# Scratch tensors in DRAM re-ordered by chunk and by head: convolved blocks, second mixer's queries and keys, attention values

## The chip, the cores and the metric

The kernel runs on one core of one Trainium2 chip. The metric is device time in microseconds (us) of one execution, the median of several; less is better. The profile is of one execution of its own, so its time stands beside the median below.

## What is computed

Two layers (`DEPTH = 2`) of a hybrid backbone, with the same weights for 128 context tokens and 1024 latent tokens. Each layer normalises, projects, runs three mixers side by side, projects back, and ends in a SwiGLU:

```python
u = rms_norm(x) * (1 + scale1) + shift1
(aq, ak, av, bq, bk, bv, bg, ba, bb, cq, ck, cv, co, ci, cf) = split(u @ w_in + b_in)
qkv = silu(centred_dwconv(concat([bq, bk, bv]), conv_w))        # 5 taps
a = diff_attention(rope(aq), [rope(ak), cached k], [av, cached v])   # 4 heads, two maps each
d = gated_delta(l2_norm(dq) / 8, l2_norm(dk), dv, beta, g)      # both directions, chunked
m = mlstm(cq, ck / 8, cv, ig, lf)                               # both directions, chunked
x += gate1 * (concat([norm(a), norm(d) * silu(bg), sigmoid(co) * norm(m)]) @ w_out)
x += gate2 * swiglu(rms_norm(x) * (1 + scale2) + shift2)
```

It returns both token streams and, for the context tokens, keys, values and the mixers' last states. Everything is float32 outside; every large product is made of three fp32r products of a high and a low part.

## The kernel before

Tokens are columns: 1152 of them (`NT`), 1024 latent and 128 context, in three groups `g` of 384 (`GW`) for the matmuls and in nine chunks of 128 (`NCH = 9`, the ninth is the context) for the mixers. A tile has 128 partitions.

Between the projections and the mixers the data goes through scratch tensors in DRAM, opened per layer in `open_s`. Three of them are the change's:

- `BT`, the convolved q, k, v blocks, `[P, 6, CVO]`: for each of 128 partitions six blocks of 1156 columns. `blk_b` (L727) stores one block `b` per call, a row of 4624 B per partition. `prep1` (L754) loads one chunk of all six blocks, six pieces of 512 B per partition. `delta_step` (L1062) loads one chunk of the first four blocks, four pieces of 512 B per partition, for either direction.
- `CQK`, queries and keys of the mLSTM mixer, `[P, 4, NT]`. `blk_c` (L746) stores block `b`, group `g`: 1536 B per partition. `prep1` (L756) loads a chunk of four blocks, four pieces of 512 B; `mlstm_step` (L1149) loads the two query blocks of a chunk, two pieces of 512 B.
- `VD`, attention values, `[10, P, 512]`: ten tiles of 128 keys by 4 heads of 128. `tok_cols` (L565) stores 256 columns (two heads) of one key tile, 1024 B per partition; `attn_consts` (L924) stores the cached values the same way. `attention` (L1231) loads one head: ten pieces of 512 B per partition.

Counts for both layers: L727 12 times, L746 24, L565 and L924 together 40; L754 and L756 18 each, L1062 and L1149 32 each, L1231 8.

The stages of a layer, in the order of the code: `tok_cols` 0 and the gates; `blk_b` and `blk_c`, ten blocks, in the first layer beside the modulation weights `aw`; `prep1` per chunk (transposes, decay matrices, stores of `RD`, `ND`, `RM`, `VK`); `inverse`; `prep2`, which loads `ND` (tile `w`, L851), finishes the triangular inverses and stores them into `RD` (L911); `blk_a` (attention's q and k, stored into `QD` and `KD`); the other `tok_cols`; then `mixers`: the scan (`delta_step`, `mlstm_step`, `merge`) beside `attention` (per head two loads of `K`, 640 KB each, one of `V`, 640 KB, and per 256 queries two of `Q`), `w_out`, and the feed-forward part.

Nearly all DMAs of the scratch are issued by SyncE (SP) in one queue, in order; weights `wr` are issued by ScalarE. The order of instructions on each engine is not that of the code: the program is built with

```python
with _tile.TileContext(nc, schedule_with_timeline_sim=True) as tc:
```

so that a planner, at build time, places every instruction by its own estimate of when operands come, and the chip then runs each engine's list as it stands. In the trace the stages above overlap: `prep1` begins among the blocks, `blk_a` and the later `tok_cols` run beside `prep1`, and attention's first scores (L1250) come among the last steps of `prep2`, ahead of the scan.

Of the kernel before, what the change touches and what calls it, by code (L numbers as in the profile page):

```python
# [17 lines left out]
P = 128  # L18
D = 1024
KB = 8  # L20
NL = 1024
NC = 128
NT = NL + NC
NG = 3
GW = 384
# [3 lines left out]
H = 4  # L29
EPS = 1e-6  # L30
NCH = 9
CVW = 1160
CVO = 1156
# [33 lines left out]
def cpos(c):  # L67
    return 128 * c if c < 8 else 1028


class Kern:
# [362 lines left out]
    def open_s(self, l):  # L434

        S = self.S = {}
        dt = lambda n, shape: self.dr.tile(shape, F32, name=f"{n}{l}")
        S["BT"] = dt("BT", [P, 6, CVO])
        S["CQK"] = dt("CQK", [P, 4, NT])
        S["V1"] = dt("V1", [NCH, P, H, 65])  # L440
        S["BC"] = dt("BC", [NCH, P, 512])
        S["QD"] = dt("QD", [8, 2, 64, NT])
        S["KD"] = dt("KD", [2, 2, 2, P, NT + P])
        S["VD"] = dt("VD", [10, P, 512])
        S["ND"] = dt("ND", [2, NCH, P, H, P])
        S["RD"] = dt("RD", [2, NCH, P, 1024])
        S["GR"] = dt("GR", [2, 16, NT])
        S["VK"] = dt("VK", [NCH, P, 768])
        S["RM"] = dt("RM", [2, NCH, P, 768])
        S["CAT"] = dt("CAT", [KB, P, NT])  # L450
        ed, pe = ExitStack(), ExitStack()
        self.dn = ed.enter_context(self.pool("psdn", PSUM))
        self.pp = pe.enter_context(self.pool("pspp", PSUM))
        return ed, pe
# [69 lines left out]
    def tok_cols(self, l, u, i, pr):  # L524

        nc, A, S = self.nc, self.A, self.S
        gb = GB if i else 10
        if i == 0:
            W = self.pre
            wd = 288  # L530
            sl = lambda w, k: w[k // 3][:, 288 * (k % 3):288 * (k % 3) + 288]
            off = 1024
            self.G = self.mx.tile([P, NCH, 32], F32, name=self.nm("G"))
        else:
            W = [self.load_w(A["w_tok"][l, i - 1, j]) for j in range(2)]
            wd = 256
            sl = lambda w, k: w[k // 4][:, 256 * (k % 4):256 * (k % 4) + 256]
            off = 256 * (i - 1)
        Wh, Wl = [w[0] for w in W], [w[1] for w in W]
        bt = self.t(pr, [P, GW], "gw", gb)  # L540
        nc.sync.dma_start(bt[:, :wd], A["btok"][l:l + 1, off:off + wd].to_broadcast([P, wd]))
        for tt in range(NCH):
            g, j = divmod(tt, 3)
            cs = slice(128 * j, 128 * j + 128)
            ps = self.ps(self.pp, "pp", 6) if i == 0 and 1 < tt < 8 else self.ps(self.dn, "dn", 2)
            o = ps[:, :wd]
            for k in range(KB):
                self.mm3(o, u[g][k][0][:, cs], u[g][k][1][:, cs], sl(Wh, k), sl(Wl, k), k == 0, k == KB - 1)
            if i == 0:
                v1 = self.t(pr, [P, GW], "gw", gb)[:, :260].rearrange("p (h v) -> p h v", h=H)  # L550
                nc.gpsimd.memset(v1[:, :, 64:65], 1.0)
                nc.vector.tensor_add(v1[:, :, 0:64], ps[:, :256].rearrange("p (h v) -> p h v", h=H),
                                     bt[:, 0:256].rearrange("p (h v) -> p h v", h=H))
                nc.sync.dma_start(S["V1"][tt], v1)
                nc.vector.tensor_add(self.G[:, tt, :], ps[:, 256:288], bt[:, 256:288])
            else:
                v = self.t(pr, [P, GW], "gw", gb)[:, :256]
                nc.vector.tensor_add(v, o, bt[:, :256])  # L558
                if i > 2:
                    nc.sync.dma_start(S["BC"][tt, :, off - 512:off - 256], v)  # L560
                    yield
                    continue
                if tt == 8:
                    nc.sync.dma_start(self.O["v"][l, :, off:off + 256], v)
                nc.sync.dma_start(S["VD"][tt if tt < 8 else 9, :, off:off + 256], v)  # L565
            yield

    def softplus(self, pool, z, shape):

# [135 lines left out]
    def blk_b(self, l, b, u):  # L705

        nc, S, pr = self.nc, self.S, self.pr
        w = self.load_w(self.A["w_st"][l, b])
        raw = self.t(self.cv, [P, CVW], "cv", 4)
        for lo, hi in ((0, 2), (1026, 1030), (1158, 1160)):  # L710
            nc.vector.memset(raw[:, lo:hi], 0.0)
        bias = self.p(l, "bst")[:, b:b + 1]
        for g in range(NG):
            ps = self.ps(self.dn, "dn", 2)
            self.block(ps[:, :GW], w, u[g])
            for lo, hi, cnd in self.ranges(g):
                o = 2 + GW * g + lo + (4 if cnd else 0)
                nc.scalar.activation(raw[:, o:o + hi - lo], ps[:, lo:hi], AF.Identity, bias=bias)
        cw = self.cwh[l]
        acc = self.t(self.cv, [P, CVW], "cv", 4)  # L720
        a = acc[:, :CVO]
        nc.vector.tensor_scalar(out=a, in0=raw[:, 0:CVO], scalar1=cw[:, 5 * b:5 * b + 1], scalar2=None, op0=ALU.mult)
        for j in range(1, 5):
            nc.vector.scalar_tensor_tensor(out=a, in0=raw[:, j:j + CVO], scalar=cw[:, 5 * b + j:5 * b + j + 1], in1=a, op0=ALU.mult, op1=ALU.add)
        nc.scalar.activation(raw[:, :CVO], a, AF.Tanh)
        nc.vector.scalar_tensor_tensor(out=a, in0=raw[:, :CVO], scalar=1.0, in1=a, op0=ALU.add, op1=ALU.mult)
        nc.sync.dma_start(S["BT"][:, b, :], a)  # L727
        if b < 4:
            sq = raw
            nc.scalar.activation(sq[:, :CVO], a, AF.Square)  # L730
            ps = self.ps(self.pp, "pp", 6)
            for c in range(NCH):
                nc.tensor.matmul(ps[:, 2 * c:2 * c + 2], lhsT=sq[:, cpos(c):cpos(c) + 128], rhs=self.hsel, start=True, stop=True)
            nc.vector.tensor_copy(self.ss[:, :, 2 * b:2 * b + 2], ps[:, :18].rearrange("p (c i) -> p c i", i=2))

    def blk_c(self, l, b, u):
        nc, S, pr = self.nc, self.S, self.pr
        w = self.load_w(self.A["w_st"][l, 6 + b])
        bias = self.p(l, "bst")[:, 6 + b:7 + b]
        for g in range(NG):  # L740
            ps = self.ps(self.dn, "dn", 2)
            self.block(ps[:, :GW], w, u[g])
            o = self.t(pr, [P, GW], "gw", GB)
            nc.scalar.activation(o, ps[:, :GW], AF.Identity, bias=bias)
            c = slice(GW * g, GW * g + GW)
            nc.sync.dma_start(S["CQK"][:, b, c], o)  # L746

    def prep1(self, l, c, c1):

        nc, S, pr, pp = self.nc, self.S, self.ch, self.pp  # L750
        o = slice(cpos(c), cpos(c) + 128)
        oc = slice(128 * c, 128 * c + 128)
        q6 = self.t(self.cv, [P, CVW], "cv", 4)[:, :768].rearrange("p (a t) -> p a t", t=128)
        nc.sync.dma_start(q6, S["BT"][:, :, o])  # L754
        c4 = self.t(c1, [P, 4, 128], "c4", 1)
        nc.sync.dma_start(c4, S["CQK"][:, :, oc])  # L756
        cq, ck = c4[:, 0:2], c4[:, 2:4]

        b4 = lambda a, w=64: a[:, :, None].to_broadcast([P, H, w])
# [13 lines left out]
        for d in range(2):  # L773
            e = self.t(c1, [P, 768], "em", EB)
# [13 lines left out]
        for d in range(2):  # L788
            gr = self.t(c1, [2, 8, 128], "gr", 2, F32R)
            nc.sync.dma_start(gr.bitcast(F32), S["GR"][:, 8 * d:8 * d + 8, oc])  # L790
            for x in range(2):
# [6 lines left out]
                if x == 0:  # L798
# [6 lines left out]
                    for b in range(4):  # L805
                        s = slice(32 * b, 32 * b + 32)
# [107 lines left out]
    def attn_consts(self, l):  # L914
        nc, pr, S, A = self.nc, self.pr, self.S, self.A
        for hf in range(2):
            ck = self.t(pr, [P, GW], "gw", GB)[:, :256].rearrange("p (b t) -> p b t", b=2)
            nc.sync.dma_start(ck, A["ckT"][l][:, hf])
            for p in range(2):
                self.put_k(hf, p, slice(NL, NL + P), ck[:, p, :], P)  # L920
        for i in range(2):
            cv = self.t(pr, [P, GW], "gw", GB)[:, :256]
            nc.sync.dma_start(cv, A["cv"][l][:, 256 * i:256 * i + 256])
            nc.sync.dma_start(S["VD"][8, :, 256 * i:256 * i + 256], cv)  # L924
        self.nlam = self.nlams[l]

    def put(self, dst, src, w):
# [118 lines left out]
    def delta_step(self, l, cs, S0, S1, seen):  # L1046
# [12 lines left out]
        if S0 is not None:  # L1059
            qk = self.t(sc, [P, 2, 4, 128], "qk", 2)  # L1060
            for d in range(2):
                nc.sync.dma_start(qk[:, d], S["BT"][:, 0:4, cpos(cs[d]):cpos(cs[d]) + 128])  # L1062
            pk = self.ps(pz, "z", 2)
            for d in range(2):
                for p in range(2):
# [60 lines left out]
    def mlstm_step(self, l, cs, C0, C1, seen):  # L1126
# [4 lines left out]
        for d in range(2):  # L1131
# [14 lines left out]
            nd = hv(nf)  # L1146
            if C0 is not None:
                cq = self.t(sc, [P, 2, 128], "cq", 3)
                nc.sync.dma_start(cq, S["CQK"][:, 0:2, 128 * c:128 * c + 128])  # L1149
                pq = self.ps(pz, "y", 1)  # L1150
                for p in range(2):
                    nc.tensor.matmul(pq[:, 130 * p:130 * p + 130], lhsT=cq[:, p, :], rhs=C0[:, d, p, :], start=True, stop=True)
# [58 lines left out]
    def attention(self, l):  # L1211
# [11 lines left out]
        for h in range(H):  # L1223
# [4 lines left out]
                nc.sync.dma_start(k.bitcast(F32), S["KD"][h // 2].rearrange("l p r t -> (l p) r t")[:, r:r + 32, :])  # L1228
                K.append(k)
            V = self.t(at, [P, 10, 128], "V", 2)  # L1230
            nc.sync.dma_start(V, S["VD"][:, :, 128 * h:128 * h + 128].rearrange("s p e -> p s e"))  # L1231
            for q0 in range(0, NT, 256):
                nq = min(256, NT - q0)
                q = self.t(at, [P, 2, 2, 256], "Q", 2, F32R)
# [319 lines left out]
```

## Time and profile before

| | us |
|---|---|
| median of 3 runs | 3792.27 (3789.85 to 3796.47) |
| the profiled execution | 3797.68 |
| its span, first to last instruction | 3795.9 |
| TensorE (PE) matmul busy in the span | 3540.6 (93%) |
| VectorE (DVE) busy | 2295.8 (60%) |
| ScalarE (ACT) busy | 1136.6 (30%) |
| GpSimd (POOL) busy | 654.4 (17%) |
| mean granted TensorE clock | 0.954 of 2.4 GHz |

Besides the page, four views of the trace are read: a table of busy times by stretch of time; the waits of an engine, by who ended them; instructions of one engine in order of time; and the DMA queues in a stretch. An issuing instruction of a DMA on SP is shown with the time that SP spent on it; the transfer itself comes after. "Packets" are the pieces that the 16 DMA engines moved, among them 16 of under 512 B for each DMA that tell of its end.

### The profile page before, as it was taken

The numbers are of one execution on the slowest core, as the hardware profiler recorded it, in microseconds if no ns is written. First come the engines' busy times: TensorE is split into PE (matmuls) and PEld (weight loads), VectorE is DVE, ScalarE is ACT, GpSimd is POOL, SyncE is SP. The second block draws the span as 40 slices with busy tenths as digits, with TensorE's granted clock in tenths as the row PEclk, the third lists the DMA queues.
The fourth block names the chain that finished last, engine by engine and source line by source line (L and its number), as shares of the span: only waits on it lengthen the run. The fifth ranks groups of instructions, "written<-read, shape, count | busy, mean of one in ns | idle before, by whom it ended". The sixth has DMA issues, their size and how long they took to land. (4 is left out here: it accounts for less than half of the span.)

```text
span 3795.9 us, 59415 instructions
## 1 busy us (share of the span) xinstructions
PE 3540.6 (93%) x22770; PEld 3369.8 (89%) x22770; DVE 2295.8 (60%) x5361; ACT 1136.6 (30%) x2383; POOL 654.4 (17%) x903
## 2 busy tenths in 40 slices
PE   7999978997899999999999997898789999999998
PEld 6997777886899999999989877788778999999997
DVE  7896677787455566654485567477775434333435
ACT  5323315445241111111243431244553311111111
POOL 2014232355020000000020324034632000000001
PEclk8999988999999999999999999889999999999999
DMA  5377624774212222221133663467542111111111
GB/s 215 128 247 234 217 78 124 225 214 132 92 59 84 78 81 81 95 78 48 59 110 99 221 230 97 132 175 205 137 140 66 34 39 41 49 40 39 51 45 56
DMA packets 277091, 434.13 MB, mean 114 GB/s; under 512 B 24648, under 2 KB 186504, under 8 KB 276552
## 3 DMA queue, kind: packets, MB, share of 16 engines
q1 hardware_dynamic: 247576, 324.29, 27.3%
q10 hardware_dynamic: 29232, 106.05, 8.7%
q8 instruction: 180, 2.95, 0.3%
q14 instruction: 103, 0.84, 0.1%
HBM read 315.85 MB, written 114.39 MB: 113 GB/s over the span
## 5 line engine op out<-in xcount | busy, mean ns | idle before, releaser
L362 DVE SCALAR_TENSOR_TENSOR x<-pd,mod,x 128x256 f32<-128x256 f32 (+1 forms) x832 | 405.2, 514 | 597.5 <-PE pd L191 596.3
L183 ACT CAST wh<-wr 128x1024 fp32r<-128x1024 f32 (+1 forms) x219 | 229.1, 1047 | 880.3 <-PE pu L190 462.2
L184 DVE TENSOR_TENSOR wl<-wr,wh 128x1024 fp32r<-128x1024 f32 (+1 forms) x219 | 267.6, 1228 | 173.6 <-ACT wh L183 173.1
L189 PE MATMUL pd<-hh,wh 128*128 128x384 f32 x1056 | 358.8, 340 | 7.3 <-DVE x L362 5.1
L189 PE MATMUL pg<-uh,wh 128*128 128x384 f32 x1056 | 357.2, 338 | 2.6 <-ACT uh L342 2.6
L190 PE MATMUL pg<-ul,wh 128*128 128x384 f32 x1056 | 357.9, 339 | 1.4 <-DVE ul L347 1.4
L299 POOL TENSOR_TENSOR nacc<-nacc,nsq 128x384 f32<-128x384 f32 x48 | 52.1, 1086 | 1769.6 <-issue 1572.7
L190 PE MATMUL pu<-ul,wh 128*128 128x384 f32 x1056 | 355.7, 337 | 0.0
L189 PE MATMUL pu<-uh,wh 128*128 128x384 f32 x1056 | 355.6, 337 | 0.0
L190 PE MATMUL pd<-hl,wh 128*128 128x384 f32 x1056 | 354.9, 336 | 0.0
L191 PE MATMUL pg<-uh,wl 128*128 128x384 f32 x1056 | 354.7, 339 | 0.0
L191 PE MATMUL pd<-hh,wl 128*128 128x384 f32 x1056 | 353.7, 336 | 0.0
L191 PE MATMUL pu<-uh,wl 128*128 128x384 f32 x1056 | 350.7, 337 | 0.0
L189 PE MATMUL dn<-uh,wh 128*128 128x384 f32 x864 | 300.1, 347 | 5.8 <-ACT gw L956 4.4
L190 PE MATMUL dn<-ul,wh 128*128 128x384 f32 x864 | 299.0, 346 | 0.0
L191 PE MATMUL dn<-uh,wl 128*128 128x384 f32 x864 | 298.2, 345 | 0.1
L1250 PE MATMUL s<-K,Q 128*128 128x384 f32 (+1 forms) x800 | 226.3, 393 | 58.6 <-DVE e L1251 23.7
L1251 DVE TENSOR_SCALAR_CACHE_REDUCE e<-s 128x384 f32<-128x384 f32 (+1 forms) x400 | 209.8, 539 | 67.8 <-PE s L1250 64.6
L189 PEld LDWEIGHTS pd<-hh,wh 128*128 128x128 f32 x1056 | 198.4, 188 | 18.6 <-issue 7.7
L189 PE MATMUL dn<-wh,uh 128*128 128x256 f32 (+1 forms) x624 | 186.2, 298 | 26.2 <-DVE gw L558 19.8
L1250 PEld LDWEIGHTS s<-K,Q 128*128 128x128 f32 x800 | 138.3, 207 | 78.8 <-DVE e L1251 39.0
L189 PEld LDWEIGHTS pg<-uh,wh 128*128 128x128 f32 x1056 | 199.5, 189 | 4.5 <-ACT uh L342 2.8
(354 smaller groups left out, 8221.6 us busy)
## 6 DMA issues: line engine op xcount, KB each, us to landing
wr<-in_w_gu_dram ACTq DMA_DIRECT2D x88, 512.0 KB
aw<-in_w_mod_dram SPq DMA_DIRECT2D x96, 256.0 KB
wr<-in_w_dn_dram ACTq DMA_DIRECT2D x44, 512.0 KB
wr<-in_w_st_dram ACTq DMA_DIRECT2D x36, 512.0 KB
rd<-RD SPq DMA_DIRECT2D x36, 512.0 KB
aw<-in_w_mod_dram SPq DMA_DIRECT2D x32, 512.0 KB
Q<-QD SPq DMA_DIRECT2D x64, 256.0 KB
RM<-em SPq DMA_DIRECT2D x36, 384.0 KB
```

Source lines behind the costliest of these rows:

```text
L183: nc.scalar.copy(hi, r)
L184: (eng or nc.vector).tensor_tensor(out=lo, in0=r, in1=hi.bitcast(F32), op=ALU.subtract)
L189: mm(out, lhsT=wh, rhs=xh, start=start, stop=False)
L190: mm(out, lhsT=wh, rhs=xl, start=False, stop=False)
L191: mm(out, lhsT=wl, rhs=xh, start=False, stop=stop)
L299: (nc.gpsimd if k in PST else nc.vector).tensor_tensor(out=self.acc[g], in0=self.acc[g], in1=s, op=ALU.add)
L362: nc.vector.scalar_tensor_tensor(out=x[g][k][:, lo:hi], in0=ps[:, lo:hi], scalar=gate[:, k, cnd:cnd + 1], in1=x[g][k][:, lo:hi], op0=ALU.m ...
L1250: nc.tensor.matmul(p[:, :w], lhsT=q[:, m, hl, 128 * j:128 * j + 128], rhs=K[m][:, 128 * ks[0]:128 * ks[0] + w], start=hl == 0, stop=hl == 1)
L1251: nc.vector.tensor_scalar(out=e[:, GW * i:GW * i + w], in0=p[:, :w], scalar1=0.125, scalar2=None, op0=ALU.mult, op1=ALU.max, accum_out=mx[ ...
```

## The change

The three scratch tensors get the order in which they are loaded: `BT` and `CQK` by chunk first, `VD` by head first. Each load then takes one unbroken row per partition: 3072 B (L754), 2048 B (L756 and L1062), 1024 B (L1149), 5120 B (L1231). Each store is cut: a convolved block goes out as eight pieces of 512 B per partition in one DMA, and one piece for the context chunk in a second DMA; a `CQK` store is three pieces of 512 B; a values store is two. What is computed, the tiles in SBUF, their buffers and the text's order of operations are the same; `BT` has no longer the columns between latent and context tokens.

```diff
-        S["BT"] = dt("BT", [P, 6, CVO])
-        S["CQK"] = dt("CQK", [P, 4, NT])
+        S["BT"] = dt("BT", [NCH, P, 6, P])
+        S["CQK"] = dt("CQK", [NCH, P, 4, P])
...
-        S["VD"] = dt("VD", [10, P, 512])
+        S["VD"] = dt("VD", [H, P, 10, P])
...
-                nc.sync.dma_start(S["VD"][tt if tt < 8 else 9, :, off:off + 256], v)
+                self.put_v(i - 1, tt if tt < 8 else 9, v)
...
+    def put_v(self, half, s, v):
+
+        self.nc.sync.dma_start(self.S["VD"][2 * half:2 * half + 2, :, s, :].rearrange("h p e -> p h e"), v.rearrange("p (h e) -> p h e", h=2))
...
-        nc.sync.dma_start(S["BT"][:, b, :], a)
+        nc.sync.dma_start(S["BT"][0:8, :, b, :].rearrange("c p t -> p c t"), a[:, :NL].rearrange("p (c t) -> p c t", t=P))
+        nc.sync.dma_start(S["BT"][8, :, b, :], a[:, cpos(8):cpos(8) + P])
...
-            nc.sync.dma_start(S["CQK"][:, b, c], o)
+            nc.sync.dma_start(S["CQK"][3 * g:3 * g + 3, :, b, :].rearrange("c p t -> p c t"), o.rearrange("p (c t) -> p c t", t=P))
...
-        nc.sync.dma_start(q6, S["BT"][:, :, o])
+        nc.sync.dma_start(q6, S["BT"][c])
...
-        nc.sync.dma_start(c4, S["CQK"][:, :, oc])
+        nc.sync.dma_start(c4, S["CQK"][c])
...
-            nc.sync.dma_start(S["VD"][8, :, 256 * i:256 * i + 256], cv)
+            self.put_v(i, 8, cv)
...
-                nc.sync.dma_start(qk[:, d], S["BT"][:, 0:4, cpos(cs[d]):cpos(cs[d]) + 128])
+                nc.sync.dma_start(qk[:, d], S["BT"][cs[d], :, 0:4, :])
...
-                nc.sync.dma_start(cq, S["CQK"][:, 0:2, 128 * c:128 * c + 128])
+                nc.sync.dma_start(cq, S["CQK"][c, :, 0:2, :])
...
-            nc.sync.dma_start(V, S["VD"][:, :, 128 * h:128 * h + 128].rearrange("s p e -> p s e"))
+            nc.sync.dma_start(V, S["VD"][h])
```

## Rows read from the trace of the kernel before

**Rows 1.** The page: its span, and TensorE's busy time, share and instructions.
```profile
span 3795.9 us, 59415 instructions
PE 3540.6 (93%) x22770; PEld 3369.8 (89%) x22770; DVE 2295.8 (60%) x5361; ACT 1136.6 (30%) x2383; POOL 654.4 (17%) x903
```

**Rows 2.** Busy times by stretch: each engine, granted clock, DMA share, GB/s.
```profile
100.00:250.00 150.00, 148.16 (x906) 145.41 (x906) 127.33 (x214) 46.85 (x68) 1.86 (x1) 0.97 0.53 181
300.00:500.00 200.00, 184.53 (x1092) 154.65 (x1093) 133.37 (x270) 62.86 (x182) 73.69 (x137) 0.91 0.64 212
...
550.00:600.00 50.00, 33.34 (x341) 28.00 (x337) 23.54 (x78) 16.75 (x46) 3.51 (x4) 0.52 0.60 156
675.00:800.00 125.00, 115.39 (x936) 110.62 (x935) 98.22 (x332) 55.80 (x127) 53.98 (x77) 0.97 0.85 250
800.00:950.00 150.00, 123.29 (x880) 109.23 (x878) 122.28 (x395) 84.32 (x198) 94.95 (x113) 0.96 0.50 147
...
2430.00:2490.00 60.00, 43.23 (x450) 36.99 (x448) 29.98 (x98) 18.60 (x53) 4.20 (x4) 0.54 0.54 140
...
555.00:564.00 9.00, 4.72 (x80) 4.33 (x80) 2.99 (x11) 1.74 (x6) 0.00 (x0) 0.50 0.27 96
```

**Rows 3.** TensorE's waits that a DMA ended: total us, times, longest us.
```profile
PE s L1250 <- DMA Q<-QD: 17.4, 4, 7.9
PE s L1250 <- DMA K<-KD: 16.8, 3, 9.0
...
PE px L879 <- DMA w<-ND: 13.2, 3, 8.6
...
PE pp L771 <- DMA c<-CQK: 5.7, 3, 3.8
PE y L1143 <- DMA rm<-RM: 5.5, 1, 5.5
```

**Rows 4.** SP's issues in order of time, at 547 and 2425 us: start, us spent.
```profile
547.01 0.59 SPq L1228 DMA_DIRECT2D K<-KD  x1
...
548.68 0.55 SPq L1228 DMA_DIRECT2D K<-KD  x1
549.28 0.71 SPq L1231 DMA_DIRECT2D V<-VD  x1
550.04 14.62 SPq L1236 DMA_DIRECT2D Q<-QD  x2
...
2425.36 0.57 SPq L1228 DMA_DIRECT2D K<-KD  x1
...
2428.90 0.55 SPq L1228 DMA_DIRECT2D K<-KD  x1
...
2430.85 0.42 SPq L1231 DMA_DIRECT2D V<-VD  x1
2431.37 12.13 SPq L851 DMA_DIRECT2D w<-ND  x1
```

**Rows 5.** TensorE in order of time, same places: start, us, [idle before, releaser].
```profile
572.86 1.62 PE L1250 MATMUL s<-K,Q 128*128 128x384 f32 x4 [9.04 <-DMA K<-KD]
...
2448.03 0.60 PE L879 MATMUL px<-cv,w 32*32 32x32 f32 x8 [8.56 <-DMA w<-ND]
2452.30 0.44 PE L879 MATMUL px<-cv,w 32*32 32x32 f32 x5 [3.66 <-DMA w<-ND]
```

**Rows 6.** DMA queues: packets, MB, share of 16 engines; 1150 to 1700 us.
```profile
q1 hardware_dynamic: 12672, 23.07, 12.6%
```

**Rows 7.** DMA queues, 700 to 725 us: all packets by size, then SP's queue.
```profile
DMA packets 6824, 7.65 MB, mean 306 GB/s; under 512 B 481, under 2 KB 5264, under 8 KB 6819
...
q1 hardware_dynamic: 6819, 7.59, 104.1%
```

**Rows 8.** Issues by tile: count, ns on SP min/median/max, first and last start.
```profile
L754 SPq DMA_DIRECT2D cv<-BT x18: 523/562/2600, 218.2 to 2176.1; - x18
L727 SPq DMA_DIRECT2D BT<-cv x12: 319/334/358, 115.1 to 2069.6; - x12
```

More of the change, by code (lines that the diff above doesn't have):

```diff
@@ L744, in blk_c @@
             nc.scalar.activation(o, ps[:, :GW], AF.Identity, bias=bias)
-            c = slice(GW * g, GW * g + GW)
-            nc.sync.dma_start(S["CQK"][:, b, c], o)
+            nc.sync.dma_start(S["CQK"][3 * g:3 * g + 3, :, b, :].rearrange("c p t -> p c t"), o.rearrange("p (c t) -> p c t", t=P))
     def prep1(self, l, c, c1):
         nc, S, pr, pp = self.nc, self.S, self.ch, self.pp
-        o = slice(cpos(c), cpos(c) + 128)
         oc = slice(128 * c, 128 * c + 128)
         q6 = self.t(self.cv, [P, CVW], "cv", 4)[:, :768].rearrange("p (a t) -> p a t", t=128)
-        nc.sync.dma_start(q6, S["BT"][:, :, o])
+        nc.sync.dma_start(q6, S["BT"][c])
         c4 = self.t(c1, [P, 4, 128], "c4", 1)
-        nc.sync.dma_start(c4, S["CQK"][:, :, oc])
+        nc.sync.dma_start(c4, S["CQK"][c])
         cq, ck = c4[:, 0:2], c4[:, 2:4]
```

## The prediction

> **What bounds the kernel now.** The page first: TensorE (PE) is busy for 93% of the span [rows 1], so time can come only from PE's idle 255 us and from stretches in which it is granted the lower of its two clocks. The busy times by stretch tell where both lie. Between 100 and 250 us, where the convolved blocks and the mLSTM blocks are made and stored, PE is busy for 148.2 of 150 us. Where chunks are prepared (300 to 500), and in the mixers (675 to 950), it is busy for 92%, 92% and 82%, with the DMA engines 64%, 85% and 50% busy. At 550 to 600 it is busy for 33.3 of 50 us at a granted clock of 0.52, and at 2430 to 2490, the same place of the second layer, for 43.2 of 60 at 0.54 [rows 2]. There the last small products of the triangular inverses meet the first loads of attention.
>
> Then PE's waits that a DMA ended: 58.6 us on the five loads shown [rows 3]. Four of the five (Q, K, `ND`, RM) the change doesn't touch; only `CQK`'s chunk load in `prep1`, 5.7 us, is one of the loads that it merges. So the change can help chiefly by what its loads do to their neighbours in SP's queue.
>
> SP's issues in order of time show such a place twice. At 547 us SP issues two loads of K and one of V within 3 us, and then spends 14.62 us on two loads of Q; from 2425 it issues two of K and one of V, and then spends 12.13 us on one load of `ND` [rows 4]. A V load is 128 x 10 = 1280 pieces of 512 B. PE in the same places idles 9.04 us until K and Q are there, and 8.56 and 3.66 us until `ND` is [rows 5]. I read this as a queue with room for so many pieces and no more: SP stands until earlier pieces have gone. The K pair empties slowly: at 555 to 564, with little else in flight, 0.27 of the 16 engines are busy, as if it ran on four or five, at 96 GB/s [rows 2]. Its 2 x 655 KB take 1.31 MB / 96 GB/s = 13.7 us, which is the stall.
>
> The Trainium skill ("Perfetto Trace Analysis", section DMA Instruction — HWDGE (DVE, Sync)) says that the profile's time of an issue is that in which its descriptors are generated, and that a full descriptor buffer makes the engines start before this is over. By that rule the 14.62 us are a full buffer; the trace agrees, but doesn't show the buffer's size.
>
> **The price of a piece.** At 1150 to 1700 us SP's queue carries 2 KB pieces alone: 12.6% of 16 engines for 550 us is 1109 us for 23.07 MB, 48.1 ns per 1000 B [rows 6]. At 700 to 725, where most pieces are small, the queue shows 104.1%, 416 us, for 7.59 MB (packets count where they start) [rows 7]. At 48.1 ns these would take 365 us; the other 51 us, over 6819 - 481 = 6338 pieces, are 8.1 ns each. So a piece of 512 B costs 24.6 ns (no overhead) to 32.7 ns; I take 8.1 ns a piece, since that row is of the mixers.
>
> **Loads, part by part.** Pieces per load are 128 partitions times runs. L754: 18 x (768 - 128) = 11,520 fewer. L756: 18 x (512 - 128) = 6,912. L1062: 32 x 384 = 12,288. L1149: 32 x 128 = 4,096. V: 8 x 1152 = 9,216. Together 44,032 pieces x 8.1 ns / 16 engines = 22.3 us of DMA time: 9.3 in `prep1`, 8.3 in the scan, 4.7 in attention, over two layers.
>
> First, the K and V bursts, two per layer, of which the first is waited for. V's work itself shrinks little: behind K on the slow engines its 80 pieces per engine take 80 x 32.7 = 2.6 us, and eight of 5120 B 2.0. The gain is in the queue: 72 fewer pieces per engine stand there, so Q and `ND` can enter some 12 us earlier and land right behind K and V. What is next late is K, 13.7 us after its issue, which stays. So the waits of 9.04, 8.56 and 3.66 us [rows 5], 21.3 together, are the upper bound, and nothing the lower. I take a third, 7 us: K's part of these waits is the larger.
>
> Second, chunk loads. A partition's row of `CQK` costs 4 x 32.7 = 131 ns now and 2048 x 0.0481 + 8 = 107 then; of `BT`, 196 and 156: a fifth less. SP's own time on the six-run load, 562 ns against 334 for a plain store [rows 8], falls too. Of the 5.7 us of waits [rows 3] I take 2; bounds 0 and 5.7.
>
> Third, the mixers. PE's waits on K, Q and RM, less the 9.04 counted above, are 30.7 us [rows 3, 5]. The DMA engines are busy for 0.85 x 125 + 0.50 x 150 = 181 us there in a layer [rows 2], and lose (8.3 + 4.7) / 2 = 6.5 us of it, 3.6%. A like share of 30.7 is 1.1 us; if all 13 us were on the path, 13. I take 2, nearer to the share, because these waits name loads whose own pieces stay.
>
> **Stores.** 12 x (1152 - 128) = 12,288 more pieces for `BT`, 24 x 256 = 6,144 for `CQK`, 40 x 128 = 5,120 for `VD`: 23,552, or 11.9 us of DMA time, and 12 more issues of 0.33 us on SP [rows 8]. `BT` and `CQK`, 9.3 us, lie where PE is busy for 148.2 of 150 us and DMA for 53% [rows 2]: cost nothing. Without that cover it would be 12 us with the values'. No computing engine waits for the second `BT` store; SP's next issue stands behind it for 0.33 us. The values' stores hold their tile a little longer, 2 x 32.7 against 57 ns per partition, which I also set at nothing.
>
> **Sum.** 7 + 2 + 2 = 11 us less, bounds 40 less (21.3 + 5.7 + 13) and 12 more. The profiled execution took 3797.7 us, 1.8 beyond its span, and 5.4 above the median. 3797.7 - 11 = 3786.7; less 5.4, 3781.
>
> **Rivals.** *No change.* K's transfer and the compute chains set every one of those waits, the freed queue is filled by what waits for K in any case, and 3792 - 2 = 3790 comes out. For it: no PE wait in the rows names V, and 52.9 of the 58.6 us name loads left as they are [rows 3]. The Trainium skill ("DMA: Bandwidth & Descriptors", section Specifications) puts the smallest transfer for line rate at 512 B. By that rule the merged loads gain nothing and the cut stores lose nothing. The rows' 8.1 ns a piece speak a little against it. Merged rows that are moved in small pieces after all would give the same time.
>
> *Slower: a new order.* The planner sees other shapes and one more store per block, and lays all engines' lists anew. The mechanism has one place: where an inverse's last `ND` loads and attention's first K pair are issued. It decides when a K pair stands ahead of an `ND` or Q load that PE needs within the pair's 13.7 us and PE has no products of the projections left. Its price is read from 2430 to 2490: PE was busy for 43.2 us at 0.54, work of 23.3 us at full clock, so 36.7 us were lost there [rows 2]. A second such stretch in one of the layers, with part of it covered, is 25 us against the forecast's 11 less: 3781 + 25 = 3806, up to 3818. For it: both layers already have such a stretch. Against: the number of loads and their bytes stay.
>
> *Faster: a stretch goes.* If the earlier Q and `ND` keep PE from falling to the lower clock, a whole stretch is won: at 550 to 600 PE's 33.3 us at 0.52 are 17.3 at full clock, 33 us lost [rows 2]. 3792 - 33 - 4 for the other terms = 3755. PE's products around the `ND` waits are of 32 rows [rows 5] and leave it little else to do there, which speaks against.
>
> **How the numbers follow.** Forecast 0.42 (3772 to 3788), no change 0.20, slower 0.23, faster by a stretch 0.15. A measurement of this kernel can tell about 0.2% (7.6 us) from no change. Of the forecast's 0.42, 0.33 lie below 3784.7; with 0.15 that makes 0.48 faster. Slower by over 0.2%: 0.23 and 0.02 of stores that lose their cover, 0.25. The rest, 0.27, is the same. The range of 8 in 10 takes in the stretch won and most of the slower case: 3750 to 3815. The likeliest case's own range is 3772 to 3788.
>
> **What would show it.** The packets of the span fall by 44,032 - 23,552 = 20,480, less 16 for each of the 12 added DMAs. The issue behind a K pair and its V takes a few us or less, not 12 to 15; if it still takes 12, the room in the queue isn't counted in pieces, and the first term falls. PE's idle time before the first scores falls below 9 us and that before `ND` below 8.6; if it stays while SP's stall is gone, K sets it and the no-change rival holds. The `CQK` waits fall below 5.7. If attention and the last steps of the inverses stand in another order and the stretches of low clock have another length, the order decides, and my sum isn't tested by the total alone.

## The result, and the profile after

The changed kernel takes 3827.39 us (median of 4 runs, 3817.74 to 3831.16), the kernel before 3793.6 beside it: a ratio of 1.0083 (95%: 1.0066 to 1.0099), some 33 us slower, where 11 us faster was forecast. The profiled execution of the changed kernel took 3817.74 us, 20 more than that of before, so the traces show somewhat less than the medians.

The page of the changed kernel (span, busy times, packets, SP's queue), and below it the packets of the kernel before:

```profile
span 3816.0 us, 59448 instructions
...
PE 3545.0 (93%) x22770; PEld 3377.0 (88%) x22770; DVE 2294.1 (60%) x5361; ACT 1138.6 (30%) x2383; POOL 656.6 (17%) x903
...
DMA packets 256803, 434.11 MB, mean 114 GB/s; under 512 B 24840, under 2 KB 158024, under 8 KB 256264
...
q1 hardware_dynamic: 227288, 324.26, 26.9%
```

```profile
DMA packets 277091, 434.13 MB, mean 114 GB/s; under 512 B 24648, under 2 KB 186504, under 8 KB 276552
```

The packets fell by 20,288, the forecast number to the last one. PE is busy for 4 us more than before [rows 1], and idle for 271.0 us instead of 255.3 (span less busy time). So the span grew chiefly in PE's idle time, and TensorE's waits that a DMA ended tell where (total, times, longest):

```profile
PE s L1253 <- DMA Q<-QD: 52.8, 7, 11.0
...
PE px L882 <- DMA w<-ND: 16.5, 4, 7.9
...
PE s L1253 <- DMA K<-KD: 8.9, 1, 8.9
...
PE pp L774 <- DMA c<-CQK: 7.3, 1, 7.3
...
PE y L1146 <- DMA rm<-RM: 4.0, 2, 2.0
```

The waits for Q rose from 17.4 to 52.8 us, those for `CQK`, whose load was merged, from 5.7 to 7.3; those for K fell from 16.8 to 8.9 [rows 3].

SP's issues of the changed kernel in the place of [rows 4], start and us spent:

```profile
566.05 0.57 SPq L1231 DMA_DIRECT2D K<-KD  x1
...
569.21 0.56 SPq L1231 DMA_DIRECT2D K<-KD  x1
569.83 3.48 SPq L1234 DMA_DIRECT2D V<-VD  x1
573.36 5.49 SPq L1239 DMA_DIRECT2D Q<-QD  x2
```

The stall behind K, K and V is short: 5.49 us for the two Q loads instead of 14.62. What was to be freed was freed, and it bought nothing. TensorE's idle time before the first scores is 5.88 us, before `ND` 3.81 in the first layer, where [rows 5] had none, and 7.90 and 2.92 in the second.

**Where the time arises.** I added up the columns of PE's matmuls in order of time (all kernels have 6,627,596 in all) and asked when each kernel begins the first matmul beyond the columns that the kernel before had done by 280, 400, 545, 950 and 2800 us; the last column is the end of the span. The differences to the kernel before, in us (positive: later; kernels of the experiments below among them):

```
                                              280    400    545    950   2800    end
changed kernel                               +1.1  +16.3  +16.6  +32.0  +26.9  +20.1
e1  its order, old transfers                 -1.9  +10.5  +16.9  +43.1  +40.3  +33.1
q1  before, BT store in two                  -0.1  +12.3  +17.2  +33.8  +35.9  +28.9
q3  changed, the two BT stores swapped       -0.4  +15.5  +22.5  +43.3  +30.4  +28.1
e3  changed, K loads of 128 rows             -0.7  +10.9  +18.9  -15.8  -69.2  -75.5
e2  before's order, new layout               +1.1   +0.8   +2.7   +3.9   -0.9   -1.7
pvc change without its BT part               -1.6   -2.6   -0.7   -1.3   +1.0   +1.2
e4  before, K loads of 128 rows              -0.1   +1.1   -0.1  -35.3  -82.8  -82.6
```

A column isn't always the same work, and at 950 PE of the kernel before stands idle, so a difference is good to a few us only. Two places show: some 12 to 16 us between 280 and 400, in the chunk preparation of the first layer, and some 15 to 26 more in the first layer's mixers, up to 950. The first belongs to every kernel whose BT store is cut in two at the source and to no other; the second only to those of them whose K loads are slow.

### The profile page after: what moved, and what is told of

Same layout as the page of the kernel before. It is cut to its first block, busy times and chain, and to the rows that moved or that the text cites. A ratio compares the mean times of both kernels' runs of the same rounds, so it can differ in the third digit from the quotient of the medians.

```text
span 3816.0 us, 59448 instructions
## 1 busy us (share of the span) xinstructions
PE 3545.0 (93%) x22770; PEld 3377.0 (88%) x22770; DVE 2294.1 (60%) x5361; ACT 1138.6 (30%) x2383; POOL 656.6 (17%) x903
## 3 DMA queue, kind: packets, MB, share of 16 engines
q1 hardware_dynamic: 227288, 324.26, 26.9%
q8 instruction: 180, 2.95, 0.3%
## 4 chain that ended last, share of the span: by engine, by line
PE 74%; DMA 11%; DVE 10%; issue 3%; ACT 1%; POOL 1%; SPq 0%; ACTq 0%; POOLq 0%; DVEq 0%
PE pd L189 6%; PE pd L190 6%; PE pd L191 6%; PE pg L191 5%; PE pu L190 5%; PE pu L191 5%; PE pu L189 5%; PE pg L190 5%; PE pg L189 5%; PE dn L190 4%; PE dn L189 4%; PE dn L191 4%; DMA Q<-QD 2%; PE s L1253 2%; PE o L1287 2%
## 5 line engine op out<-in xcount | busy, mean ns | idle before, releaser
L1253 PE MATMUL s<-K,Q 128*128 128x384 f32 (+1 forms) x800 | 223.4, 390 | 83.4 <-DMA Q<-QD 52.8
```

The costliest lines, as they stand in the source:

```text
L1253: nc.tensor.matmul(p[:, :w], lhsT=q[:, m, hl, 128 * j:128 * j + 128], rhs=K[m][:, 128 * ks[0]:128 * ks[0] + w], start=hl == 0, stop=hl == 1)
```

## The experiments

### Order or layout?

The first two runs exchange the transfers of the two kernels after the order is fixed, so that order and layout come apart. e1 keeps the changed kernel's lists and takes the old transfers:

```diff
-S["BT"] = dt("BT", [NCH, P, 6, P])   CQK, VD likewise
+rows of 1152, stores of 4096 + 512 B a partition, loads in pieces of 512 B, in the changed kernel's order
```

> The changed kernel's order of instructions on every engine, with the old transfers put back into it: blocks, queries and keys, and values lie and are loaded and stored as in the kernel before; only the second BT store of each block (512 B a partition) stays a transfer of its own, 12 in all. If the new order alone makes the loss (theory A): 3820 to 3830, and the Q waits of about 10 us at the heads' starts stay. If the cut stores or the merged rows make it (theory B): 3790 to 3800, near the kernel before. If the merged loads do give something in the new order too, as my first term says, this kernel is slower than the changed one, by up to 11 us, and SP's long issues behind a K pair and its V come back.

Measured: 3825.41 us, ratio 1.0092 (1.0076 to 1.0108). e2 keeps the lists of before and takes the new layout:

```diff
-nc.sync.dma_start(S["BT"][:, b, :], a)
+BT, CQK, VD by chunk and head, in the order of the kernel before
```

> The kernel before, its order of instructions on every engine untouched, with the new layout in its transfers: stores cut by chunk and by head, loads merged. One difference to the change: the store of a convolved block is one transfer of nine pieces of 512 B a partition, and its ninth piece starts four columns early, so the last chunk's convolved numbers are not those of the reference; the work done on them is the same. Theory A (the order): 3782 to 3794, that is between the forecast's sum and no change, with SP's 14.62 and 12.13 us behind the K pair gone or short. Theory B (the layout itself costs): 3815 to 3830.

Measured: 3795.99 us beside 3792.12, ratio 1.0006 (0.9992 to 1.0019). That is 2 us above its expected range. So the order (with the second BT stores, which e1 keeps) makes the whole of the loss, and the layout by itself moves nothing that can be measured, in either order. In e2 the stall of [rows 4] is gone, and PE's wait stays. SP's issue, TensorE's first scores and its `ND` wait, all of e2:

```profile
552.69 5.28 SPq L1236 DMA_DIRECT2D Q<-QD  x2
```

```profile
575.29 1.62 PE L1250 MATMUL s<-K,Q 128*128 128x384 f32 x4 [8.70 <-DMA Q<-QD]
```

```profile
PE px L879 <- DMA w<-ND: 12.3, 3, 8.0
```

8.70 us instead of 9.04, and 12.3 us for `ND` instead of 13.2: Q and `ND` enter the queue earlier and land no earlier, since the K pair is in front of them on the engines that it uses. That is the no-change rival, measured in its own place.

### Which part lays the new order?

q1 is the kernel before with one edit, and pvc the change without that part.

```diff
-        nc.sync.dma_start(S["BT"][:, b, :], a)
+        nc.sync.dma_start(S["BT"][:, b, 0:NL], a[:, 0:NL])
+        nc.sync.dma_start(S["BT"][:, b, NL:CVO], a[:, NL:CVO])
```

> The kernel before with one edit at the source: the store of a convolved block into BT is cut into two transfers (columns 0 to 1023, and the other 132), layout and all loads as before. Written out for PE and VectorE, the planner's order with this edit is that of the changed kernel, row for row. Theory A (the order that the second store brings about makes the loss): 3815 to 3832, slower by 0.6 to 1.0%, with Q waits of about 50 us. Rival (the loss needs the other parts of the change, or their loads): under 3805.

Measured: 3829.17 us, ratio 1.0100 (1.0086 to 1.0113); Q waits 49.2 us.

```diff
-S["BT"] = dt("BT", [NCH, P, 6, P]), its two stores and its merged loads
+S["BT"] = dt("BT", [P, 6, CVO]), one store, loads in pieces
```

> The change without its BT part: queries and keys by chunk, values by head, BT as before. PE's and VectorE's orders are those of the kernel before, row for row; SyncE's list differs a little. Theory A: 3782 to 3796, no loss, and if the queue's stall behind the K pair was worth something, up to 10 us faster. Rival (cut stores or SyncE's own list cost): 3800 to 3825.

Measured: 3796.58 us beside 3791.78, ratio 1.0012 (1.0002 to 1.0022), 0.6 us above its expected range and under 0.3% in any case. So twelve store issues of 0.4 to 0.6 us, which no engine waits for, bring all of the 33 us, through the planner. Of PE's 22,770 matmuls the first 1544 stand as before, and then another order comes; q1's list for PE is the changed kernel's from end to end. No run has the second stores in the old order, so the stores themselves are parted from the order only by time: q1 has issued all six of the first layer by 216 us and is level with the kernel before at 280; the lateness comes after 293, where the lists part. Which engine's list carries it isn't parted either. Why a store moves so much is in the planner's estimates, which no trace shows. Swapping the two stores gives a third order:

```diff
-store of chunks 0 to 7, then store of chunk 8
+store of chunk 8, then store of chunks 0 to 7
```

> The changed kernel with the two stores of a convolved block swapped, the chunk of the context first: the same transfers, another order laid by the planner. If what makes the loss is how that one order happens to place the K pairs against PE's work (theory A), another order gives another time anywhere in 3785 to 3830, and its Q, K and ND waits move with it. If any order with the cut stores loses (rival: one more issue on SP per block), 3820 to 3832 again.

Measured: 3824.37 us, ratio 1.0083 (1.0068 to 1.0099), Q waits 38.4 us. Another order, the same loss: the rival's number, though not shown to be for its reason, since both orders have the same two places.

### What do the Q waits wait for?

The prediction had read a K pair as running "on four or five" engines. Here each K load reads 128 rows that lie one behind the other, in both orders:

```diff
-S["KD"][h // 2].rearrange("l p r t -> (l p) r t")[:, r:r + 32, :]      # 4 groups of 32 rows
+128 consecutive rows of 5120 B, order untouched
```

> The changed kernel, order untouched, with each K load of attention reading 128 rows that lie one behind the other in KD (the same 655 KB in rows of 5120 B, but not the keys that the head needs, so the scores are those of other keys) instead of four groups of 32 rows. Theory C (a K load runs on four of the 16 DMA engines, and the Q load behind the pair waits for that): the DMA engines' busy share behind a K pair rises from 0.27 towards 1, a Q load behind it lands in 4 to 6 us instead of 13 to 15, the Q waits of 52.8 us fall below 20, and the time falls by 30 to 45 us, to 3780 to 3797. If the first Q waits for its own store or for room in the queue (rival), the waits stay and the time moves by less than 8 us.

> The kernel before, order untouched, with the same other K loads (128 rows one behind the other, the same bytes, other keys). Theory C: the 14.62 and 12.13 us of SP behind the K pair and V fall to a few us, PE's 9.04 us before the first scores falls, and of the K, Q and ND waits (47.3 us) about half goes: 3765 to 3780. Rival (K's engines do not matter): within 8 us of the kernel before. If V's 1280 pieces fill the queue whatever K does, the 12 to 15 us issues stay.

Measured: 3726.31 us on the changed kernel (ratio 0.9829, 0.9812 to 0.9846) and 3715.09 on the kernel before (0.9807, 0.9788 to 0.9826). That is 101 and 77 us, more than either expectation. On the kernel before, the waits for Q, K and `ND` fell by 40 us (47.4 to 7.0), about half of the gain. The waits for Q of the two kernels, e3 first:

```profile
PE s L1253 <- DMA Q<-QD: 3.8, 3, 2.1
```

```profile
PE s L1250 <- DMA Q<-QD: 5.2, 4, 4.4
```

Where the rest is, e4's page tells:

```profile
span 3713.3 us, 59415 instructions
...
PE 3527.2 (95%) x22770; PEld 3357.5 (90%) x22770; DVE 2296.9 (62%) x5361; ACT 1138.6 (31%) x2383; POOL 654.4 (18%) x903
```

The span is 82.6 us shorter than in [rows 1]: PE's idle time fell from 255.3 to 186.1 us, its busy time by 13.4. So 69 us are idle time: the 40 above, the 5.5 of `RM`, and some 23 in other, smaller waits, which no run ties to the K loads one by one. The 13 go with the clock: the mean granted clock of e4 is 0.965 instead of 0.954.

Between the two orders 11 us are left of 33. So some 22 of the new order's 33 us pass through the K loads. Whether the four groups are slow for their number or for their distance in DRAM, e5 asks: the addresses of e4, written as 4 groups of 32.

```diff
-128 rows
+[[40960, 4], [1280, 32], [1, 1280]], the same bytes
```

> The kernel before, order untouched. Each K load reads 128 consecutive rows of KD as in the run of the kernel before with consecutive rows (other keys than the head needs), so the addresses are the same as there, but the transfer is written as 4 groups of 32 rows, as the kernel before writes it. Theory C (the outermost count of 4 of the pattern puts the load on four engines): 3784 to 3800, the gain of 77 us is gone, and the DMA share behind a K pair is 0.25 to 0.3 again. Rival (the distance of the four groups in DRAM makes the load slow): 3710 to 3725.

Measured: 3793.66 us, ratio 1.0 (0.9987 to 1.0014): the whole gain is gone, at the same addresses. Busy times in the K pair's stretch, e5 and then e4 (the last three columns are granted clock, DMA share, GB/s):

```profile
552.00:558.00 6.00, 4.08 (x77) 3.79 (x76) 2.66 (x10) 1.18 (x4) 0.00 (x0) 0.50 0.28 107
```

```profile
549.00:558.00 9.00, 8.58 (x153) 7.82 (x149) 5.93 (x20) 2.37 (x8) 0.00 (x0) 0.59 1.07 307
```

0.28 of 16 engines is four and a half, at 107 GB/s; with 128 rows outermost all are busy, at 307. The packets of the two pages, e5 and then e4, give the number:

```profile
DMA packets 277091, 434.13 MB, mean 115 GB/s; under 512 B 24648, under 2 KB 186504, under 8 KB 276552
```

```profile
DMA packets 277283, 434.13 MB, mean 117 GB/s; under 512 B 24840, under 2 KB 186696, under 8 KB 276744
```

e4 has 192 small packets more, 12 for each of the 16 K loads. The twelve DMAs that the change adds brought 16 each, 192 in all. If a K load of e4 has 16 too, one of e5 and of the kernel before (24648 as well) has four: one for each engine, if four engines carry it, as the share says. The Trainium skill ("DMA: Bandwidth & Descriptors", section Rules for kernel authors) states this: an outermost dimension smaller than 16 confines a DMA to at most so many engines. The trace agrees, with some 75 us between e4 and e5 (ratios 0.9807 and 1.0). I had read the four engines off the trace and treated them as given. e4's loads differ from e5's also in the form of their issue (0.32 to 0.48 us of SP against 0.55 to 0.59); s3b below, with the addresses of the kernel before, 32 outermost and 0.5 to 0.6 us an issue, is fast too.

### By which placement?

In the changed order the second K load of five heads is issued ahead of half of the head's first Q, at the fourth and the sixth of the eight heads ahead of all of it. SP and TensorE of the changed kernel at its fourth head:

```profile
884.81 0.56 SPq L1231 DMA_DIRECT2D K<-KD  x1
885.42 0.61 SPq L1239 DMA_DIRECT2D Q<-QD  x1
...
886.73 4.22 SPq L1239 DMA_DIRECT2D Q<-QD  x3
```

```profile
901.29 1.01 PE L1253 MATMUL s<-K,Q 128*128 128x384 f32 x2 [10.28 <-DMA Q<-QD]
```

The kernel before at the same head, both halves of Q ahead of K:

```profile
843.58 0.59 SPq L1236 DMA_DIRECT2D Q<-QD  x1
...
847.12 0.58 SPq L1236 DMA_DIRECT2D Q<-QD  x1
...
848.45 0.56 SPq L1228 DMA_DIRECT2D K<-KD  x1
```

```profile
851.76 0.79 PE L1250 MATMUL s<-K,Q 128*128 128x384 f32 x3 [0.84 <-DMA Q<-QD]
```

Summed over the eight heads, PE waits 52.5 us before a head's first scores in the changed kernel and 26.9 in the kernel before. The next run moves five K issues, and nothing else (where K stood ahead of both halves of Q, the first half takes over K's wait for PE):

```diff
 Q (first half)
-K (second map)
 Q (second half)
+K (second map)
```

> The changed kernel with five issues moved on SP and nothing else: at heads 1, 2, 3 (first layer), 5 and 7 (second layer: the second and the fourth head) the second K load of the head stands behind both halves of its first Q load, not ahead of the last one; all other lists, row for row, and all transfers are the changed kernel's. If Q behind K is the placement that loses (theory D): the Q waits fall from 52.8 to under 20, the first scores (map 0) start 8 to 11 us earlier, part of that comes back as waits for K at the scores of map 1, and the time falls by 10 to 25 us, to 3800 to 3818. If the K load's own lateness sets it wherever Q stands (rival): the Q waits turn into K waits of about the same sum, and the time moves by less than 6 us.

Measured: 3819.19 us, ratio 1.0065 (1.0052 to 1.0078), 7 to 10 us less than the changed kernel, by ratio or by difference to the kernel before, with intervals that overlap. That lies between the two expected ranges. The waits before the first scores fell from 52.5 to 5.7, and others came. TensorE's waits of this kernel:

```profile
PE s L1253 <- DMA K<-KD: 28.0, 6, 7.7
PE y L1146 <- DMA rm<-RM: 22.2, 2, 15.8
...
PE z L1070 <- DMA qk<-BT: 7.8, 1, 7.8
...
PE s L1253 <- DMA Q<-QD: 5.6, 1, 5.6
```

All waits that a DMA ended come to 87.2 us, against 92.5 in the changed kernel. So the rival is nearer: where Q stands decides which wait it is, and hardly how much is waited. What is issued behind a K load on four engines is late, here the `RM` load issued 0.6 us after one, for which PE stood 15.8 us; with K on all engines no wait for `RM` or `BT`'s chunk is left (e3, e4).

### K loads on all engines, with the keys that are needed

Four transfers of 32 rows per K load, on both kernels; `KD` laid out by head, on the changed one; and two transfers with rows in the order (row, half), for which Q's rows are stored in the same order:

```diff
+for lp in range(4):                                              # s1b on before, s1a on the changed kernel
+    nc.sync.dma_start(k[32 * lp:32 * lp + 32, :].bitcast(F32), S["KD"][h // 2, lp // 2, lp % 2, r:r + 32, :])
...
+S["KD"] = dt("KD", [2, 4, 2, 2, 32, NT + P])                     # s2a: load S["KD"][h // 2, r // 32], keys stored in two
...
+for l2 in range(2):                                              # s3b on before, s3a on the changed kernel
+    nc.sync.dma_start(k[64 * l2:64 * l2 + 64, :].bitcast(F32), S["KD"][h // 2, l2, :, r:r + 32, :].rearrange("p r t -> r p t"))
```

> The kernel before with each K load cut into four transfers of 32 rows, at the source: the keys needed, nothing left out, 48 more issues on SP (0.3 to 0.6 us each, some 20 us of SP in all, which is not the bound), and the planner's order laid anew. Theory C: the Q, K and ND waits fall from 47 us to under 15 and the time is 3705 to 3745, faster than before by 1.2 to 2.3%. If a new order by itself costs as much as the change's did with fast K loads (about 11 us), the upper end. Rival (the K load is slow for its addresses): 3785 to 3830.

> The changed kernel with the same four transfers per K load, order laid anew. Theory C: 3705 to 3745, and the change's loss against the same edit on the kernel before shrinks from 33 us to under 20. Rival (addresses): 3800 to 3840.

> The changed kernel with KD laid out by head as well, at the source: each K load reads 128 consecutive rows in one transfer (all 16 engines), while each store of keys becomes two transfers of four groups of 32 rows (40 stores become 80, each some 197 KB or less on four engines, 2 us at 96 GB/s). Nothing is left out; order laid anew. Theory C: 3710 to 3750, if the stores on four engines lie beside full PE. If they hold up the first K loads, the waits before the first scores are 5 us or more, and the time is 3750 to 3780.

> The kernel before with each K load as two transfers, one for the high and one for the low parts, whose rows are taken in the order (row of 32, half) so that the outermost count is 32; the query rows in QD are stored in the same order, so the products are the same and nothing is left out. 16 issues more on SP, not 48; order laid anew. Theory C: as fast as four transfers or faster, 3705 to 3745. Rival (16 engines are not reached with an outermost count of 32 in 64 rows): 3785 to 3800.

> The whole change with the same K loads of two transfers; nothing is left out, order laid anew. With fast K loads the order matters less: 3735 to 3752, within 12 us of the kernel before with the same K loads (3740). If the second BT store's order costs by itself: 3760 to 3780.

Measured: s1b 3744.44 us (0.9866, 0.9839 to 0.9893), s1a 3739.03 (0.9857, 0.9833 to 0.9881), s2a 3752.73 (0.9890, 0.9868 to 0.9912), s3b 3739.86 (0.9866, 0.9853 to 0.9880), s3a 3740.33 (0.9852, 0.9834 to 0.9870). The change's loss is gone in both pairs (s1a against s1b, s3a against s3b), though the cut BT stores still make the first layer's chunk preparation 16 to 18 us later at 545 us. s2a, with its keys stored from four groups, is the slowest and the latest there, by 36 us at 545; it has the time of its second case without that case's sign, since PE waits 1.1 us before the first scores and not 5. The other four lie in their ranges. The DMA engines behind s3b's first K pair:

```profile
549.00:552.00 3.00, 3.00 (x45) 2.78 (x46) 1.65 (x5) 0.56 (x2) 0.00 (x0) 0.67 1.05 286
```

All engines are busy, at 286 GB/s, with the keys that are needed. These kernels gain 43 to 57 us, not e4's 77; their orders are new, and what the difference is due to isn't shown (s3b has 19.9 us of Q waits left, e4 5.2).

The last is s3b with the change's CQK and VD parts:

```diff
+s3b's K loads
+CQK by chunk, VD by head
```

> The kernel before with K loads of two transfers whose outermost count is 32 (query rows stored in the same order), and the change's CQK and VD parts, BT as before; nothing is left out. PE's order is that of the same kernel without the CQK and VD parts, which took 3740. If merged loads give something once K is fast: 3725 to 3738. If not: 3738 to 3748.

Measured: 3737.14 us, ratio 0.9851 (0.9835 to 0.9866): the lowest of these, 1.5% faster than before and 2.4% faster than the changed kernel, but not to be told from s1a, s3a or s3b.

## Why the prediction was wrong, point by point

**The step that failed** is in the stores: the second BT store was set at 0.33 us of SP, since no computing engine waits for it. The term was looked for on SP, and it is in the order: with that store in the program the planner lays other lists, and those cost the 33 us, in q1 with that edit alone. Up to 280 us, with all six stores of the first layer issued, q1 is no later than before. I had the planner's new order among the rivals, but for the sum I kept the order of before.

**The slower rival** had the sign and, for its larger part, the mechanism: a K load ahead of a load that PE needs within its 13.7 us. Its place was wrong. It looked at the start of attention, with the first K pair; there the changed kernel waits in the first layer 5.88 us for Q and 3.81 for `ND`, against 9.04 and none before, and so hardly more. The waits came at the second, third and fourth head, and in the second layer at the second and fourth. Its price of 25 us was near the 22 that pass through the K loads, five places together; that is luck, since it was read from a stretch at the start of attention. And it was counted from 3781, with a gain of 11 that did not come: from 3792 it is 3817. The 11 us that remain to the 3827 measured are those that the two orders keep with fast K loads, and the range, which ended at 3815, held neither.

**The other place of the loss** was in no case. The changed kernel's first chunk preparation, 290 to 350 us, and that of before:

```profile
290.00:350.00 60.00, 49.99 (x222) 40.53 (x221) 34.59 (x64) 18.36 (x50) 20.70 (x29) 0.80 0.60 202
```

```profile
290.00:350.00 60.00, 53.10 (x263) 44.03 (x262) 41.58 (x74) 22.17 (x58) 22.69 (x32) 0.89 0.69 233
```

PE is busy 3 us less, and at a granted clock of 0.80 instead of 0.89. In the changed kernel it waits in one piece for the merged load and, 30 us later, for VectorE's `em`, before it can begin a decay matrix:

```profile
301.50 0.69 PE L774 MATMUL pp<-con,c 128*128 128x128 f32 x2 [7.26 <-DMA c<-CQK]
...
331.19 0.77 PE L796 MATMUL pp<-neg,idr 128*128 128x512 f32 x1 [2.75 <-DVE em L778]
```

The kernel before waits in the same place for ScalarE and then for the same load:

```profile
300.78 0.44 PE L189 MATMUL dn<-uh,wh 128*128 128x384 f32 x1 [2.95 <-ACT gw L956]
...
306.89 0.69 PE L771 MATMUL pp<-con,c 128*128 128x128 f32 x2 [3.76 <-DMA c<-CQK]
```

The load took less in the change: issued at 296.62, PE could go on 4.9 us later, against 299.52 and 7.4 before. PE had less work laid in front of it: at the chunk's first matmul the two lists part, and the kernel before has 36 products of the projections ahead of it. But in length the 7.26 us stand against 2.95 + 3.76 = 6.71; the larger difference is the wait for `em`, between 280 and 420 us, changed kernel and then before:

```profile
PE pp L796 <- DVE em L778: 8.5, 3, 4.8
```

```profile
PE pp L793 <- DVE em L775: 2.2, 3, 1.3
```
Both waits are longer in all nine kernels with the cut store (over the whole span 6.7 to 8.4 us for `CQK` and 12.3 to 19.9 for `em`, 23.0 in s2a) than in the eight without it (2.2 to 5.7 and 7.7 to 10.7). That they bring the lower clock and the rest of the lateness is only argued, and no run took them away alone.

**First term, 7 us (0 to 21.3):** the queue's room was read rightly. Both the V load's 1280 pieces and a slow K are needed for the stall: it shrinks when V is merged (e2: 5.28 us) and when K is fast and V is not (e4: 2.56 us for the same two Q loads), and stays where neither is done (e5: 13.25). But its end was worth nothing. I had named K as what is next late, and then taken a third of the waits all the same; e2 shows that K sets nearly all of them.

**Second and third term, 2 and 2 us:** in e2, the order of before, the `CQK` waits fell from 5.7 to 4.1 us, those for K and Q together from 34.2 to 33.3, and `RM` rose from 5.5 to 6.7. The sum, 11 us less, came out as 2 us more (3 less to 7 more, by the interval of e2's ratio). The no-change rival's 3790 was right for the layout.

**The price of a piece** was of the right size: e1 has 22,016 pieces more than the changed kernel in SP's queue (249,304 against 227,288), and the times of all that queue's packets add up to 134 us more, 6.1 ns each, against the 8.1 forecast. (The pages' shares, 26.9% over 3816 us and 27.1% over 3829, would give 8.1, but are rounded too coarsely to tell.) The 22.3 us of loads and 11.9 us of stores that were worked out from it moved no time that can be measured (e2).

**The stores' cover** held: e2 has every cut store, a block's nine pieces in one transfer, and loses nothing that can be measured.

**The faster rival** did not come: around the first scores, at 570 to 620 us, the changed kernel's granted clock is 0.50, as low as in [rows 2].

## What to carry to other kernels

Where a planner lays the lists, first ask what an edit adds to the lists, and forecast the time with the old order and with a new one as two cases; when the result is in, put the old transfers into the new order and the new transfers into the old one, and the two come apart in one comparison. Before costing what stands behind a slow transfer, ask why it is slow: here the outermost count of 4 in K's pattern was worth 77 us in the order of before, and 43 to 58 in kernels that load the keys they need. Merging what stands behind it gained nothing that can be measured, with K slow (e2) or fast (s3v against s3b).

## What the runs showed of the hardware

- Behind loads of 655 KB whose pattern has 4 as its outermost count, 0.28 of 16 DMA engines are busy (107 GB/s); with the same bytes and 128 outermost all engines are busy (307 GB/s with the loads behind it), and a load has 12 small packets more. The time of the whole kernel differs by some 75 us (e5, e4). So not every DMA has the same number of packets that tell of its end.
- What is issued behind a load on four engines is late: PE waited 11.0 us for a Q (changed kernel), 8.6 for `ND` (before), and, with the five K issues moved, 15.8 for `RM` and 7.8 for `BT`'s chunk. With K on all engines and the order untouched these waits are gone or small (e3: at most 2.1 us for Q, none for the others; e4: 4.4 for Q, 1.0 for `ND`).
- More than the named waits went with the slow load. With 40 us less of Q, K and `ND` waits the kernel before took 77 us less; in the profiled executions PE's idle time fell by 69 us, and its busy time by 13, with the mean granted clock up from 0.954 to 0.965 (e4).
- 44,032 load pieces fewer and 23,552 store pieces more, together 20,480 packets fewer in the order of before, changed the time by +0.06% (-0.08 to +0.19%; e2).
